# Max-pooling 134 MB through one core: loads first, stores last, issued from GpSimd with the single-packet option

## The chip, the cores and the metric

One core of a Trainium2 chip. The metric is the device time of a run in microseconds (us); the runs of one kernel lie at most 0.26% apart (number 14; 0.18% or less in all others). Besides the run times there is a profile of one run of each kernel; its span is 1.8 to 2.3 us shorter than the time of the run.

## The reference

The input is 32 x 256 x 4096 float32 (134.22 MB). Each row of 4096 is cut into 256 windows of 16 elements, and the largest of each is kept. The output is 32 x 256 x 256 float32 (8.39 MB).

```python
for i in range(output_size):                      # 256
    start = int(i * length / output_size)
    end = int((i + 1) * length / output_size)
    result[:, :, i] = np.max(x[:, :, start:end], axis=-1)
```

That is one pass over memory: 142.6 MB moved, and one VectorE reduction for each of 64 tiles of 128 rows.

## The kernel before

The 8192 rows are 64 tiles of 128 partitions. A ring in SBUF holds nine tiles, and a load brings three, so three loads fit. The output is collected in six buffers of nine tiles each and stored in large pieces. Two stores leave ScalarE's queue amid the loads; five are held back and issued from SyncE after the loads, to give the DMA engines work while VectorE finishes. The last loads get smaller (`LATE`, `PIECES`) so that little is left to reduce after the last byte has come.

```python
RING = 9; G = 9; N_GROUPS = 7; LOAD = 3
LATE = [3, 2, 2, 1, 1]; HELD = 4; PIECES = 4
# ... (views of input and output, buffers)
for g in range(N_GROUPS):
    o = outs[g % len(outs)]
    sizes = LATE if g == N_GROUPS - 1 else [LOAD] * (G // LOAD)
    r = 0
    for n in sizes:
        at = n_read % RING
        nc.sync.dma_start(out=ring[:, at : at + n], in_=xg[g][:, r : r + n])
        for i in range(n):
            nc.vector.reduce_max(out=o[:, (r + i) * O : (r + i + 1) * O],
                                 in_=ring[:, at + i], axis=mybir.AxisListType.X)
        n_read += n
        r += n
    if g < N_GROUPS - 1 - HELD:
        nc.scalar.dma_start(out=og[g], in_=o)
    else:
        held.append((og[g], o))
# ... (the 64th tile in four pieces)
for dst, src in held:
    nc.sync.dma_start(out=dst, in_=src)
nc.scalar.dma_start(out=ol, in_=last_out)
```

## Time and profile before

336.75 us (median of 3 runs, 336.65 to 336.76). What matters of it:

| | before |
|---|---|
| span of the profile | 334.8 us |
| bytes moved | 142.62 MB |
| VectorE busy | 278.8 us |
| three reductions of a load | 13.08 us |
| a load of 6.29 MB at the steady 433 GB/s | 14.5 us |
| first reduction starts | 17.79 us |

The head of the page of the kernel before. A digit is the busy share of one fortieth of the span in tenths; the row GB/s is what DMA moved in it.

```profile
span 334.8 us, 174 instructions
...
DVE  0088989885988959798988989898898988999992
...
DMA  9899999999998999899998999989999999999997
GB/s 370 382 470 446 399 470 393 461 386 439 435 464 382 429 464 464 382 470 423 423 470 376 470 452 393 470 382 464 452 393 470 399 446 431 435 416 411 411 433 315
DMA packets 5041, 142.62 MB, mean 426 GB/s; under 512 B 560, under 2 KB 688, under 8 KB 1200
```

DMA has no empty slice. VectorE (DVE) starts in the third slice and then has a small gap in every load's turn: DMA bounds this kernel, and VectorE needs 10% less time for a load (13.08 us against 14.5).

The chain that ended last of the kernel before, in order of time: start, duration, and what was waited for or run.

```profile
0.66 0.07 issue
0.73 17.04 DMA ring<-in_x_dram
17.77 0.02 issue
17.79 13.08 DVE out L65 x3
30.88 0.02 issue
30.89 30.46 DMA ring<-in_x_dram
```

The first load lands at 17.77 us. Its three reductions end at 30.88, which frees its third of the ring for load 4; that one lands 30.46 us later, because one full load is queued ahead of it. A freed third of the ring thus turns into a request about one load's time before DMA would run out.

Two terms before the next view. A descriptor is one piece of a transfer: the trace shows a load of three tiles as 128 pieces of 48 KB, eight on each of the 16 DMA engines, and calls each of them a packet. A transfer lands when the semaphore that tells of its end has its last update.

The DMA issues of the page before, with the median time from issue to landing in the last column:

```profile
ring<-in_x_dram SPq DMA_DIRECT2D x19, 6144.0 KB, 30.5
...
out_dram<-out ACTq DMA_DIRECT2D x2, 1152.0 KB, 21.5
```

A store of 1152 KB would need 2.7 us alone at 433 GB/s; beside SyncE's loads it needs 21.5 (the median of two), because on each DMA engine its eight descriptors take turns with 48 KB load descriptors, as the packet records show.

### The profile page before, as it was taken

What the parts mean: (1) busy time and instruction counts of PE and PEld (TensorE: products, weight loads), DVE (VectorE), ACT (ScalarE), POOL (GpSimd) and SP (SyncE); (2) the same over time, 40 slices, a digit from 0 to 9 for tenths busy, and PEclk for the clock granted to TensorE, in tenths of its full rate; (3) what the DMA queues carried; (4) which work ended last, traced back from release to release, by engine and by line L of the source; (5) the groups of instructions that cost most, each with busy time, mean ns of one, the idle gap of its engine ahead of it and who ended that gap; (6) DMA issues with size and microseconds to landing.
All of it is one profiled execution on the core that took longest, in us unless ns stands there. A gap on an engine that the chain in (4) does not pass through costs nothing.

```text
span 334.8 us, 174 instructions
## 1 busy us (share of the span) xinstructions
DVE 278.8 (83%) x67; POOL 0.2 (0%) x4
## 2 busy tenths in 40 slices
DVE  0088989885988959798988989898898988999992
POOL 0000000000000000000000000000000000000000
DMA  9899999999998999899998999989999999999997
GB/s 370 382 470 446 399 470 393 461 386 439 435 464 382 429 464 464 382 470 423 423 470 376 470 452 393 470 382 464 452 393 470 399 446 431 435 416 411 411 433 315
DMA packets 5041, 142.62 MB, mean 426 GB/s; under 512 B 560, under 2 KB 688, under 8 KB 1200
## 3 DMA queue, kind: packets, MB, share of 16 engines
q1 hardware_dynamic: 4608, 140.12, 97.4%
q10 hardware_dynamic: 432, 2.49, 1.8%
q14 instruction: 1, 0.01, 0.0%
HBM read 134.22 MB, written 8.39 MB: 426 GB/s over the span
## 4 chain that ended last, share of the span: by engine, by line
DMA 61%; DVE 34%; issue 2%; DVEq 0%
DMA ring<-in_x_dram 61%; DVE out L65 33%; DVE lastout L82 1%; DVEq L119 0%; DVEq L65 0%
## 5 line engine op out<-in xcount | busy, mean ns | idle before, releaser
L65 DVE TENSOR_REDUCE out<-ring 128x256 f32<-128x4096 f32 x63 | 274.3, 4412 | 50.0 <-DMA ring<-in_x_dram 50.0
L82 DVE TENSOR_REDUCE lastout<-ring 128x64 f32<-128x1024 f32 x4 | 4.6, 1208 | 0.0
L105 POOL MEMSET const-bfloat16-1.0<- 128x1 bf16 x1 | 0.1, 102 | 0.0
L105 POOL MEMSET const-uint8-127<- 128x1 uint8 x1 | 0.1, 102 | 0.0
L105 POOL MEMSET const-float32-0.0<- 128x1 f32 x1 | 0.1, 99 | 0.2 <-issue 0.2
L105 POOL MEMSET const-float32-1.0<- 128x1 f32 x1 | 0.1, 99 | 0.0
## 6 DMA issues: line engine op xcount, KB each, us to landing
ring<-in_x_dram SPq DMA_DIRECT2D x19, 6144.0 KB, 30.5
ring<-in_x_dram SPq DMA_DIRECT2D x2, 4096.0 KB, 30.0
out_dram<-out SPq DMA_DIRECT2D x5, 1152.0 KB, 14.8
ring<-in_x_dram SPq DMA_DIRECT2D x2, 2048.0 KB, 30.9
out_dram<-out ACTq DMA_DIRECT2D x2, 1152.0 KB, 21.5
ring<-in_x_dram SPq DMA_DIRECT2D x4, 512.0 KB, 27.8
out_dram<-lastout ACTq DMA_DIRECT2D x1, 128.0 KB, 5.2
```

The lines of the kernel that those rows point to most:

```text
L65: nc.vector.reduce_max(out=o[:, (r + i) * O : (r + i + 1) * O], in_=ring[:, at + i], axis=mybir.AxisListType.X,)
L82: nc.vector.reduce_max(out=last_out[:, cut], in_=ring[:, at, cut], axis=mybir.AxisListType.X)
L105: nc = _bacc.Bacc("TRN2", target_bir_lowering=False, num_devices=1)
```

## The change

Its intent: one queue, so that all loads come before all stores and 19 us of stores (8.39 MB at 433 GB/s) cover the last reductions; large, equal transfers; the option `single_packet=True`; and the first load from SyncE, whose first byte came at 1.74 us. The 64th tile's result goes to a spare part of the ring.

```diff
-    G = 9
-    N_GROUPS = 7
+    G = 21
+    N_GROUPS = 3
     LOAD = 3
-    LATE = [3, 2, 2, 1, 1]
-    HELD = 4
-    PIECES = 4
+    CUT = 15
 ... (buffers; pooled() is the reduce_max of before)
+    def move(dst, src):
+        if n_read == 0:
+            nc.sync.dma_start(out=dst, in_=src)
+        else:
+            nc.gpsimd.dma_start(out=dst, in_=src, single_packet=True)
 ...
     for g in range(N_GROUPS):
 ...
+        for r in range(0, G, LOAD):
             at = n_read % RING
-            nc.sync.dma_start(out=ring[:, at : at + n], in_=xg[g][:, r : r + n])
 ...
+            move(ring[:, at : at + LOAD], xg[g][:, r : r + LOAD])
+            for i in range(LOAD):
+                pooled(outs[g][:, (r + i) * O : (r + i + 1) * O], ring[:, at + i])
+            n_read += LOAD
 ...
+    move(ring[:, at], xl)
+    pooled(spare, ring[:, at])
 ...
-    for dst, src in held:
-        nc.sync.dma_start(out=dst, in_=src)
-    nc.scalar.dma_start(out=ol, in_=last_out)
+    for g in range(N_GROUPS - 1):
+        move(og[g], outs[g])
+    for a, b in ((0, CUT), (CUT, G)):
+        move(og[N_GROUPS - 1][:, a * O : b * O],
+             outs[N_GROUPS - 1][:, a * O : b * O])
+    nc.scalar.dma_start(out=ol, in_=spare)
```

More of the change, by code (lines that the diff above doesn't have):

```diff
@@ L44 @@
         pool.tile([P, G * O], fp32, tag=f"out{i}", name=f"out{i}")
-        for i in range(N_GROUPS - 1)
+        for i in range(N_GROUPS)
     ]
-    last_out = pool.tile([P, O], fp32, tag="lastout", name="lastout")
     main = N_GROUPS * G * P
@@ L53, with pooled @@
     ol = of[main:rows]
+    def pooled(dst, src):
+        nc.vector.reduce_max(out=dst, in_=src, axis=mybir.AxisListType.X)
+    def move(dst, src):
[3 more added lines that the diff above has]
+            nc.gpsimd.dma_start(out=dst, in_=src, single_packet=True)
     n_read = 0
-    held = []
     for g in range(N_GROUPS):
-        o = outs[g % len(outs)]
-        sizes = LATE if g == N_GROUPS - 1 else [LOAD] * (G // LOAD)
-        r = 0
-        for n in sizes:
+        for r in range(0, G, LOAD):
             at = n_read % RING
-            nc.sync.dma_start(out=ring[:, at : at + n], in_=xg[g][:, r : r + n])
-            for i in range(n):
-                nc.vector.reduce_max(
-                    out=o[:, (r + i) * O : (r + i + 1) * O],
-                    in_=ring[:, at + i],
-                    axis=mybir.AxisListType.X,
-                )
-            n_read += n
-            r += n
-        if g < N_GROUPS - 1 - HELD:
-            nc.scalar.dma_start(out=og[g], in_=o)
-        else:
-            held.append((og[g], o))
-    at = n_read % RING
-    oc = O // PIECES
-    for c in range(PIECES):
-        cut = slice(c * oc, (c + 1) * oc)
-        nc.sync.dma_start(out=ring[:, at, cut], in_=xl[:, cut])
-        nc.vector.reduce_max(
-            out=last_out[:, cut], in_=ring[:, at, cut], axis=mybir.AxisListType.X
-        )
-    for dst, src in held:
-        nc.sync.dma_start(out=dst, in_=src)
-    nc.scalar.dma_start(out=ol, in_=last_out)
+            move(ring[:, at : at + LOAD], xg[g][:, r : r + LOAD])
+            for i in range(LOAD):
+                pooled(outs[g][:, (r + i) * O : (r + i + 1) * O], ring[:, at + i])
+            n_read += LOAD
+    at = n_read % RING
+    spare = ring[:, (at + LOAD) % RING].rearrange("p o w -> p (o w)")[:, 0:O]
+    move(ring[:, at], xl)
[3 more added lines that the diff above has]
+    for a, b in ((0, CUT), (CUT, G)):
+        move(
+            og[N_GROUPS - 1][:, a * O : b * O],
+            outs[N_GROUPS - 1][:, a * O : b * O],
+        )
+    nc.scalar.dma_start(out=ol, in_=spare)
 _INS = ['x', 'output_size']
```

## The prediction

> **What bounds it now.** The DMA engines. The page's slices show DMA busy 9 or more tenths nearly everywhere; in the table by stretches 20 to 280 us run at 433 GB/s with a DMA share of 1.00. 142.62 MB at that rate are 329.1 us of a span of 334.8; only 5.7 us are not transfer: the start (the first load, issued at 0.73 us, lands at 17.8; its bytes need 14.5) and a thin end (330 to 335 us: share 0.55). VectorE is second: 64 tiles x 4.41 us = 282 us; the three reductions of a load take 13.1 us, a load 14.5 us.
>
> **What the change can win.** Same bytes, so at most about 5 us. (a) Packets: the trace's packet records show 1815 ns for 49152 B, 347 for 9216 B, 159 for 4096 B. These fit 27.2 GB/s plus about 8 ns a packet; with 288 packets per engine, one packet per transfer might save 2 us (estimate). (b) Tail: the stores (8.39 MB, 19.3 us at 433 GB/s) follow the last load and cover the last reductions (13.2 + 4.4 us), so the end should be dense: 1 to 2 us.
>
> **What it adds.** The first load is on SyncE's queue, eight packets per DMA engine of 1.8 us; loads 2 and 3 come from GpSimd with nothing to wait for[...]. [...] beside ScalarE's first store, 9 KB packets alternate one for one with 48 KB load packets, and a 1.15 MB store needs 21.5 us to land. [...] Load 1, which VectorE wants first, lands last, at about 46.5 us instead of 17.8. The ring holds three loads, so load 4 can't be issued until load 1 is reduced: 46.5 + 13.1 = 59.6, plus 1.5 to start. DMA stands idle about 14.7 us. All of it is on the critical path. Afterwards DMA is continuous: 123.7 MB at 434.5 GB/s = 284.8 us from 61.2, ends at 346.0, plus 0.8 of closing: span 346.8. Measured time is 1.8 above the span: **348.5 us**.
>
> **Other outcome.** [...] there is no hole: about 333 to 335 us. I give this 40%.
>
> Range 332.5 to 351 (it has to cover both). Faster by over 2%: 0.04; within 2%: 0.38; slower: 0.58.
>
> **What would show it.** First reduction's start: about 46 us (right) or 18 us (other outcome), about 31 us if queues alternate by descriptor. A hole of 13 to 15 us in the DMA slices near 46 to 61 us. Steady rate 433 to 435.2 GB/s. Stores alone after the last load, near 420 to 435 GB/s, full to the end.
>
> **What would make it wrong.** A late GpSimd start; arbitration by descriptor; a software queue that is slower than 433 GB/s, or an engine lagging under it, which costs 3.3 us per per cent; stores alone slower than mixed with loads.

The two conditions of the other outcome were other turns or a late GpSimd. The sum: load 1 lands at about 46.5 us, then 13.1 for its reductions and 1.5 to start again give about 61.2; 284.8 for the other bytes gives 346.0, 0.8 of closing 346.8, and 1.8 outside the span 348.5 us. The 46.5 is my estimate, not shown by a trace: three loads of 14.5 us and about 3 us of start (the first load's 17.8 less its 14.5), if load 1 lands last. The 1.5 was an estimate too; number 5 shows 1.53, from the end of load 1's reductions (60.72) to the next packet (62.25).

## The result, and the profile after

337.51 us (median of 6 runs, 337.24 to 337.73) against 336.70 of the kernel before beside it (336.60 to 336.76). The ratio is 1.0023, 95% interval 1.001 to 1.0036: the same within 2%, and slower by a small, certain amount. Ratios here are the mean time of one kernel's runs over that of the other's of the same rounds, so they are not quite the ratio of the medians quoted.

The head of the page after:

```profile
span 335.4 us, 158 instructions
...
DVE  0003999999999999989898898989789898988990
...
DMA  9899899989999999899999999999989999999996
GB/s 369 387 463 457 387 446 399 463 387 463 440 405 469 410 434 463 387 463 434 410 469 393 451 451 393 469 417 428 463 381 469 428 416 463 393 457 399 441 422 271
DMA packets 3889, 142.62 MB, mean 425 GB/s; under 512 B 432, under 2 KB 560, under 8 KB 688
```

There is no hole in the row DMA. VectorE starts a slice later than before and is then full for 13 slices.

The chain after, its first pieces and the load that follows:

```profile
0.74 30.18 DMA ring<-in_x_dram
30.92 0.02 issue
30.94 116.92 DVE out L53 x27
147.86 0.28 issue
148.14 30.04 DMA ring<-in_x_dram
```

The first load, alone on SyncE's queue, lands at 30.92 us. VectorE then runs 27 reductions without a wait. It is late by 13 us and, being about 1.4 us faster per load than DMA, works that off over nine loads. After that the kernel has the old rhythm.

The timeline after, up to 60 us (start, duration, engine, line, instruction; in brackets the idle time before it):

```profile
0.74 0.37 SPq L57 DMA_DIRECT2D ring<-in_x_dram  x1
1.28 1.20 POOL L59 DMA_DIRECT2D ring<-in_x_dram  x2 [0.84 <-PEq L113]
30.94 30.38 DVE L53 TENSOR_REDUCE out<-ring 128x256 f32<-128x4096 f32 x7 [30.94 <-DMA ring<-in_x_dram]
44.31 0.53 POOL L59 DMA_DIRECT2D ring<-in_x_dram  x1 [41.83 <-DVE out L53]
```

GpSimd had issued loads 2 and 3 by 2.5 us, as foreseen. Load 4 went out at 44.31 us; load 3 landed at 47.3. So the next request was there 3 us ahead, and DMA never starved.

The trace's records of single DMA packets show the order on an engine. Strung together by their end and start times (H: a 48 KB descriptor from SyncE's queue, P: one from GpSimd's), the first 24 packets of each of the 16 engines in the kernel after read

```
HHPHPHPHPHPHPHPPPPPPPPPP
```

Each engine took one descriptor from either queue in turn, although P belongs to transfers issued with `single_packet=True`. The first P began at 5.82 us, and the last H ended at 30.55.

Where the rest went shows in four times from those records, placed in the span (us):

| | first byte | last byte | transfer, first to last byte | tail, last byte to end of span |
|---|---|---|---|---|
| before | 1.74 | 333.63 | 331.89 | 1.15 |
| after | 1.74 | 333.20 | 331.46 | 2.15 |

The transfers as a whole became 0.43 us shorter and the tail 1.00 us longer. In the tail after, the trace's instruction records show a drain instruction on GpSimd (one of the program's closing instructions) that ends at 334.63, 1.07 us after the last landing at 333.56; the closing barrier of all engines comes only then. In the kernel before, the barrier follows the last landing directly (334.14 after 333.97). Together the two make the span 0.57 us longer; the measured time differs by 0.81. The profiled runs differ outside the span too: time less span is 1.78 us before and 2.16 after. What that is, the profile does not show. Below it is 2.0 to 2.3 us in the runs that issue most transfers from GpSimd, except in numbers 11 (1.78) and 13 (1.77), which ran on other chips than numbers 1 to 8; so it cannot be read as a price of GpSimd's queue.

The expectations of numbers 3, 4 and 8 count the tail from the last landing instead (0.81 us before, 1.79 after); those from number 9 on count it from the last byte, as the table does.

### The profile page after: what moved, and what is told of

The parts are those of the page before. It is cut to its first block, busy times and chain, and to the rows that moved or that the text cites. A ratio compares the mean times of both kernels' runs of the same rounds, so it can differ in the third digit from the quotient of the medians.

```text
span 335.4 us, 158 instructions
## 1 busy us (share of the span) xinstructions
DVE 278.1 (83%) x64; POOL 13.5 (4%) x29
## 2 busy tenths in 40 slices
DMA packets 3889, 142.62 MB, mean 425 GB/s; under 512 B 432, under 2 KB 560, under 8 KB 688
## 3 DMA queue, kind: packets, MB, share of 16 engines
HBM read 134.22 MB, written 8.39 MB: 425 GB/s over the span
## 4 chain that ended last, share of the span: by engine, by line
DVE 49%; DMA 45%; DVEq 2%; issue 0%
DVE out L53 48%; DMA ring<-in_x_dram 45%; DVEq L113 2%; DVE ring L53 1%
## 5 line engine op out<-in xcount | busy, mean ns | idle before, releaser
L59 POOL DMA_DIRECT2D ring<-in_x_dram x21 | 11.2, 535 | 273.8 <-DVE out L53 273.0
L53 DVE TENSOR_REDUCE ring<-ring 128x256 f32<-128x4096 f32 x1 | 4.4, 4408 | 0.0
L59 POOL DMA_DIRECT2D out_dram<-out x4 | 2.1, 534 | 35.6 <-DVE out L53 35.6
```

What stands on the lines that cost most here:

```text
L53: nc.vector.reduce_max(out=dst, in_=src, axis=mybir.AxisListType.X)
L59: nc.gpsimd.dma_start(out=dst, in_=src, single_packet=True)
```

## The experiments

Theory A, formed on this result: a DMA engine takes turns between two queues one descriptor at a time, and asking for a single packet changes nothing in that. Its rival is the order that I had assumed (load 1 last), or a framing that does something else. Theory C: the lost microsecond is GpSimd's drain. Its rivals are D, a fixed price of using GpSimd's queue at all, and E, a price that grows with the number of its transfers.

### 1. Without the one-packet option

```diff
-            nc.gpsimd.dma_start(out=dst, in_=src, single_packet=True)
+            nc.gpsimd.dma_start(out=dst, in_=src)
```

> The changed kernel without the one-packet option. Theory A (an engine takes turns by descriptor, whatever the framing): nothing moves; first reduction at 31 us, 337.5 us within 0.3, 1815 ns per 48 KB. Rival B (the framing does something, only not what I predicted, for example saves a gap per descriptor): 338 to 340 us, or another order of the first three loads.

Measured: 337.57 us (337.41 to 337.62), first reduction at 30.65 us. Nothing moved beyond 0.3 us. At this size the option is worth nothing, in order or in time.

### 2. First load from GpSimd too

```diff
-        if n_read == 0:
-            nc.sync.dma_start(out=dst, in_=src)
-        else:
-            nc.gpsimd.dma_start(out=dst, in_=src, single_packet=True)
+        nc.gpsimd.dma_start(out=dst, in_=src, single_packet=True)
```

> The changed kernel with the first load from GpSimd too, so one queue for all. Theory A: load 1 is no longer shared with 2 and 3 and lands at 18 to 19 us, VectorE starts 12 us earlier, yet the time hardly moves, because DMA was never idle in the changed kernel: 337.5 to 338.5, the later first byte (about 0.9 us) being all that is lost. Rival (the late first reduction costs time): 2 us or more faster than the changed kernel.

Measured: 338.02 us (337.95 to 338.07). The first byte came at 2.65 us (issue at 1.28) instead of 1.74, and the first reduction began at 19.19 us instead of 30.94. VectorE started 12 us sooner and the kernel ended half a microsecond later: a late start of the engine that has slack cost nothing here. "The first load from SyncE" is worth 0.5 us, less than the 0.92 by which the first byte comes sooner: from first to last byte this run took 331.17 us, 0.29 less than the changed kernel.

### 3. The new order, all from SyncE

```diff
-        if n_read == 0:
-            nc.sync.dma_start(out=dst, in_=src)
-        else:
-            nc.gpsimd.dma_start(out=dst, in_=src, single_packet=True)
+        nc.sync.dma_start(out=dst, in_=src)
```

> The changed order, all from SyncE (last store from ScalarE as in the change). Theory C (the change loses about 1 us at the end because GpSimd's closing drain runs 1.07 us beyond the last landing, and gains 0.4 us of transfer by fewer, larger descriptors): tail after the last byte about 0.8 us, span 334.4, time 336.2 to 336.4, so 0.3 to 0.4 us faster than before. Rival (software issue makes the transfers themselves slower): DMA from first to last byte would shorten below 331.3 us.

Measured: 336.03 us (335.89 to 336.12), ratio to before 0.9979 (0.9967 to 0.9992). First to last byte 331.22 us, tail 1.29 (0.93 from the last landing), span 334.24, time less span 1.79. It beats both kernels, the changed one by 1.5 us. The transfers were 0.24 us shorter than the changed kernel's. By its letter this is the rival's sign (under 331.3), but number 2, where GpSimd issues all loads, has 331.17: software issue does not make the transfers slower. The shorter time goes with one queue at the start: with 48 KB descriptors the runs of this order that begin on one queue have 331.08 to 331.22 (numbers 2, 3, 10), those that begin on two 331.44 to 331.61 (the changed kernel, 1, 4, 11). The tail and the time outside the span make the rest. The page of this kernel:

```profile
DVE  0088989898898989989898898989889898988990
...
DMA  9899898998989989999899998999989999898997
```

VectorE starts in the third slice again. The order is the changed kernel's, only the issuer differs.

### 4. Last piece of the store from SyncE

```diff
-    for a, b in ((0, CUT), (CUT, G)):
-        move(og[N_GROUPS - 1][:, a * O : b * O], ...)
+    move(og2[:, 0 : CUT * O], o2[:, 0 : CUT * O])
+    nc.sync.dma_start(out=og2[:, CUT * O : G * O], in_=o2[:, CUT * O : G * O])
```

> The changed kernel, only the last piece of a store from SyncE, so that GpSimd's last transfer lands about 1.5 us before the end. Theory C: the drain is over before the last landing; tail 0.8 us instead of 1.8, time 336.4 to 336.7. Rival (the second of tail is a fixed price of having used GpSimd's queue at all): 337.4 to 337.6.

Measured: 337.31 us (337.13 to 337.65), tail 1.93. This looks like rival D, but the experiment missed its aim: the piece on SyncE took turns with GpSimd's piece, so GpSimd's last transfer did not land 1.5 us before the end but at 333.56, as late as ever. It decides nothing. Number 11 repairs it.

### 5. SyncE's first load in 8 KB descriptors

```diff
-            nc.sync.dma_start(out=dst, in_=src)
+            nc.sync.dma_start(out=dst, in_=src, max_dma_last_dim=8192)
```

> The changed kernel, only SyncE's first load cut into 8 KB descriptors (48 per engine). Theory A (turn by turn, one descriptor each): load 1 gets 8 KB per turn against 48 KB of loads 2 and 3, so those finish at about 36 us and load 1 last, at about 46 us; load 4 is issued at about 59.5, DMA idles 13 to 15 us, span about 349, time 350 to 352: the hole of my prediction, made by other means. Rival (turns are shared by bytes, or loads 2 and 3 don't matter): load 1 at 31 us or earlier, about 337.5 us.

Measured: 354.49 us (354.19 to 354.56), ratio 1.0527. Load 1 landed at 47.6 us, load 4 was issued at 61.0. In the chain that ended last, load 1 is this piece:

```profile
0.74 46.87 DMA ring<-in_x_dram
```

Stretches of this run (start:end, length, VectorE busy, GpSimd busy, clock, DMA share, GB/s):

```profile
40.00:45.00 5.00, 0.00 (x0) 0.00 (x0) 1.00 1.01 421
45.00:50.00 5.00, 2.36 (x1) 0.00 (x0) 1.00 0.27 110
50.00:55.00 5.00, 5.00 (x2) 0.00 (x0) 1.00 0.00 0
55.00:60.00 5.00, 5.00 (x2) 0.00 (x0) 1.00 0.00 0
60.00:65.00 5.00, 5.00 (x3) 0.53 (x1) 1.00 0.70 246
```

This is the forecast hole: two stretches in which DMA moved nothing while VectorE worked. By the packet records no engine had a packet from 47.19 to 62.25 us, 15.1 us long. Nothing was changed but the size of the first load's descriptors, and with it what this load gets per turn; the packets, strung together as above, again alternate one for one. First to last byte became 348.05 us, 16.6 longer than in the changed kernel. Theory A's times for load 1 and for the issue hold within 1.6 us. Loads 2 and 3 landed at 23.8 and 41.1, not both at about 36: they share a queue and came one after the other, and some ten small descriptors of load 1 went before the first of theirs. The time came out 2.5 us above the range; the hole is at the upper end of what I had put, and where the other 1.5 us of longer transfer come from was not traced.

### 6 and 7. GpSimd's transfers in 8 KB descriptors, with and without the one-packet option

```diff
-            nc.gpsimd.dma_start(out=dst, in_=src, single_packet=True)
+            nc.gpsimd.dma_start(
+                out=dst, in_=src, single_packet=True, max_dma_last_dim=8192   # 7: single_packet=False
+            )
```

> The changed kernel with GpSimd's transfers cut into 8 KB descriptors, 48 per engine[...]. Theory A: load 1 is hardly delayed, 8 x (1.8 + 0.3) + 2 = about 19.5 us. My prediction's mechanism [...] would put it at about 46 us with a hole, over 350 us. Cost of descriptors: if each costs 8 ns whatever the framing, about 40 more per engine and load add 6 to 7 us: 344 us; if the framing saves it, 337.5.

> As the run before, without the one-packet option. Theory A: the same as with it: load 1 at about 19.5 us, about 344 us. If the framing matters for small descriptors, this run and the one before differ, in the landing of load 1 or by several us of time.

Measured: 344.43 us (344.28 to 344.46) with the option, 344.40 (344.20 to 344.51) without. First reduction at 20.26 and 20.54 us. The page of the run with the option:

```profile
DVE  0069989789797978979797897979789797977990
...
DMA  8989999999999999999999999999999999999997
...
DMA packets 17457, 142.62 MB, mean 417 GB/s; under 512 B 432, under 2 KB 560, under 8 KB 1712
```

What VectorE waited for in it: us in total, times, the longest, which is the wait for load 1.

```profile
DVE out L53 <- DMA ring<-in_x_dram: 55.3, 20, 20.3
```

The prediction's order would have put load 1 last, at about 46 us. It landed at 20.2 with the option and at 20.5 without, where theory A's turns of one descriptor each gave about 19.5. The option saves nothing on descriptors either: first to last byte grew by 7.56 us over the changed kernel (339.03 against 331.46). By the packet counts of the two pages an engine had (17457 - 3889) / 16 = 848 descriptors more, so each cost 8.9 ns.

### 8. The kernel before, issued from GpSimd

```diff
-            nc.sync.dma_start(...)      # everywhere
+            nc.gpsimd.dma_start(...)
```

> The kernel before, with everything that SyncE issues moved to GpSimd (the order, pieces and ScalarE stores kept). Theory C: the drain ends the kernel, tail 1.7 to 1.9 us instead of 0.8, and the first byte comes some tenths later: 337.6 to 338.8. Rival (the queue costs nothing, the new order costs): 336.7 within 0.2.

Measured: 339.04 us (339.02 to 339.06), ratio 1.0067. First byte at 2.66, first to last byte 331.85 (before: 331.89), tail 2.24 (1.87 from the last landing, as theory C had), time less span 2.28. The transfers are as fast as from SyncE. The price is 0.92 us at the first byte, 1.09 of tail and 0.50 outside the span; the time came out 0.2 us higher than I had allowed.

### 9. One load in the middle from GpSimd, the rest from SyncE

```diff
-        nc.sync.dma_start(out=dst, in_=src)
+        if n_read == 30:
+            nc.gpsimd.dma_start(out=dst, in_=src)
+        else:
+            nc.sync.dma_start(out=dst, in_=src)
```

> All from SyncE (336.03 us) with one load in the middle moved to GpSimd. Theory C (the second at the end is GpSimd's drain after its own last landing): that landing is 170 us before the end, so the tail stays at 1.2 to 1.3 us and the span at 334.2 to 334.4; time 336.0 to 336.2. Rival D (a fixed price for having used GpSimd's queue at all): tail 2.1 us, time 337 or more.

Measured: 345.90 us (345.71 to 346.34), which neither theory had. The tail is as theory C said, 1.30 us, with the drain over at 166.65, 0.08 us after the one landing. The 10 us have another cause: this run makes the collision in the middle of the kernel, and it changed the order of VectorE's work there.

```profile
150.00:165.00 15.00, 0.00 (x0) 0.00 (x0) 1.00 0.98 423
165.00:175.00 10.00, 8.41 (x2) 0.00 (x0) 1.00 1.06 457
175.00:185.00 10.00, 10.00 (x4) 0.00 (x0) 1.00 0.13 44
```

VectorE's next work in the timeline, with the idle time before it:

```profile
166.59 56.34 DVE L53 TENSOR_REDUCE out<-ring 128x256 f32<-128x4096 f32 x13 [19.03 <-DMA ring<-in_x_dram]
```

SyncE's load issued at 118.5 shared its turns with GpSimd's, issued at 133.3, and landed at 161.7 instead of 149.0 (all from SyncE). In addition the instruction records show that VectorE's program had one reduction of GpSimd's load ahead of those of the load before it, so it waited to 166.59. The third of the ring came free at 184.0. By the packet records the engines had run empty between 176.5 and 177.6, and none had a packet from 177.61 to 184.98.

The collision alone would probably not have made this hole. Had VectorE begun with the load of 161.7, its three reductions (13.08 us) would have freed the third at 174.8, and SyncE's next transfer, 1.0 us from issue to first byte, would have reached the engines at about 175.8, before any ran empty. This is an estimate from the numbers above; no run has the collision without the changed order, and why the built program has that order the record does not show. So two loads that shared the turns made the landing 12.7 us late; that DMA then starved took, by this estimate, the further 9.2 us that VectorE's order cost. At the start of the changed kernel, where VectorE took the loads in order, the request came 3 us before load 3 landed.

### 10. Only the last piece of the store from GpSimd

```diff
     # all from SyncE (number 3), except
+    nc.gpsimd.dma_start(out=og2[:, CUT * O : G * O], in_=o2[:, CUT * O : G * O])
```

> All from SyncE with only the last piece of the stores (0.8 MB) moved to GpSimd, so one transfer, but one of the last to land. Theory C: tail 1.9 to 2.3 us, span 335.0 to 335.4, time 336.9 to 337.4. Rival E (the price grows with the number of GpSimd's transfers, 25 in the changed kernel): 336.1.

Measured: 336.03 us (335.92 to 336.27), tail 1.33. GpSimd's transfer landed at 333.06, among the last, and the drain ended at 333.14. This is rival E's figure. Theory C in its fixed form fell, and so did D.

### 11. Both last pieces from SyncE

```diff
-    for a, b in ((0, CUT), (CUT, G)):
-        move(og[N_GROUPS - 1][:, a * O : b * O], ...)
+    for a, b in ((CUT, G), (0, CUT)):
+        nc.sync.dma_start(out=og2[:, a * O : b * O], in_=o2[:, a * O : b * O])
```

> The changed kernel, with both pieces of the last group's store from SyncE, the piece that is ready last first, so that GpSimd's last transfer lands some 4 us before the end. Theory C: GpSimd's drain is over before SyncE's last landing, tail 1.2 to 1.3 us, time 336.4 to 336.8. Rival D: tail 2.1, time 337.5.

Measured: 336.17 us (335.99 to 336.20), ratio 0.9983, tail 1.24. GpSimd issued 23 transfers, the last landed at 331.87, and its drain ran 0.99 us more, to 332.86. SyncE's and ScalarE's last landings are at 333.24 and 333.56, so the drain hid behind them. This is the changed kernel with two transfers moved, and 1.3 us faster, from different rounds and 0.2 us better than I had put. In the profiled runs 0.91 of it is tail; 0.38 lies outside the span, and as this run was on another chip than number 1, the changed kernel but for the option, that part need not come from the edit. The lag is there, but here it cost only as far as it outlasted the last landing of all the queues (in number 4 it did, though GpSimd's was not the last).

### 12. The first store amid the loads

```diff
     # all from SyncE, except, after the last tile of group 0:
+        if g == 0:
+            nc.scalar.dma_start(out=og[0], in_=outs[0])
     # ... (its store after the loads is left out)
```

> All from SyncE, but the first 2.75 MB store leaves from ScalarE as soon as it is reduced, amid the loads. If the loads-first order is worth something by itself: loads end 6.3 us later, the last reductions at about 333 us and the last small store lands after them with little left to cover it: 337.5 to 339. Rival (order is worth nothing here, DMA is busy either way): 336.0 within 0.2.

Measured: 337.75 us (337.60 to 337.79). The last reduction ended at 333.2, the small last store was issued at 333.26 and landed at 334.97, when everything else had landed by 333.44. The packet records have no gap amid the loads, and one at the end, from 333.03 to 334.11. So loads first is worth 1.7 us in this version (336.03 of number 3, from other rounds). The kernel before got the same cover in another way, with five held stores and ever smaller last loads; that is probably why the change gains almost nothing by it.

### 13. One row per transfer

```diff
-    LOAD = 3
+    LOAD = 1
```

> The changed kernel with one row (16 KB descriptors) per transfer, so 67 transfers from GpSimd instead of 25. Rival E (about 43 ns of drain per GpSimd transfer): the drain ends 2.8 to 3.0 us after GpSimd's last landing, tail about 4 us. Theory C (fixed): 1.0 to 1.1 us after, tail 2.2. Either way the smaller descriptors add 16 per engine and three rows, 21 times, at 8 ns: about 2.7 us of transfer. Time with E about 342, with C about 340.

Measured: 341.97 us (341.81 to 342.10). GpSimd issued 67 transfers, and the drain ended 2.78 us after the last landing. First to last byte is 334.52, which is 3.06 longer than the changed kernel's. Rival E's figure again. Over the runs, the lag of the drain against GpSimd's number of transfers:

| run | transfers from GpSimd | drain's end after their last landing, us |
|---|---|---|
| 9, 10 | 1 | 0.08 |
| 11 | 23 | 0.99 |
| 4 | 24 | 1.03 |
| changed kernel, 1, 5 | 25 | 1.07 |
| 2 | 26 | 1.11 |
| 8 | 32 | 1.35 |
| 13 | 67 | 2.78 |
| 6, 7 (8 KB descriptors) | 25 | 0.46 |

The first seven rows lie on 0.04 us plus 0.041 per transfer. The last row does not. Its loads have six times the descriptors, and why its lag is smaller was not tested.

### 14. The middle load from ScalarE

```diff
         if n_read == 30:
-            nc.gpsimd.dma_start(out=dst, in_=src)
+            nc.scalar.dma_start(out=dst, in_=src)
```

> All from SyncE with one load in the middle from ScalarE. If two hardware queues take turns by descriptor just as SyncE's and GpSimd's did: the load before it, issued at 118.5, lands at about 162 instead of 149 us, VectorE waits for both, and the time is 345 to 347 as with GpSimd. Rival (only the software queue pushes in): 336.0 to 336.3.

Measured: 345.66 us (345.39 to 346.28). The load before it landed at 161.8, not at 149.0 as in number 3, and VectorE waited 18.8 us, again for the later of the two loads first, as in number 9. Taking turns does not belong to the software queue; ScalarE's queue does it too.

## Why the prediction was wrong

The measured 337.5 us lies inside the wide range, but the forecast was 348.5 and "slower", and that was wrong. That it lies inside is no merit: the range had to cover two outcomes, and the measured time is neither of them.

**The step that failed** reads: "Load 1, which VectorE wants first, lands last, at about 46.5 us instead of 17.8." It rested on an assumption of mine about the order of turns, which no trace showed, and on my reading of the diff that a transfer goes as a single packet. The runs showed one descriptor of each in turn. Load 1 needs eight turns, load 2 too, so they landed at 30.9 and 32.7 us and load 3 at 47.3. Load 1 was indeed late, by 13 us, but not by 29. Numbers 1, 6 and 7 show no trace of such a packet: with the option and without it the first reduction began at 30.94 and 30.65 us (48 KB descriptors), and at 20.26 and 20.54 (8 KB). Whether the framing is not made, or made and not honoured in the order of turns, these runs cannot tell.

**What followed from it was right.** Number 5 gave load 1 the late landing by other means: 47.6 us (foreseen 46.5), load 4 at 61.0, an empty DMA, and a time 17 us longer. The chain "load 1 late, ring full, DMA idle" held there. Its input was false. In total the prediction's own steps would have fallen 6 us short of number 5 (348.5 against 354.5): its transfers began again 1.1 us later than foreseen, took 287.6 us from there and not 284.8, and the tail and the time outside the span were 1.7 us longer.

**The other outcome was mis-sized as well.** I gave it 333 to 335 us. Three terms were off:

- (a) "one packet per transfer might save 2 us (estimate)": 0 us (numbers 1, and 6 against 7). The 8 ns of the fit, 8.9 in number 6, are paid for each descriptor.
- (b) "Tail: ... 1 to 2 us": the last byte came 0.43 us sooner. I read the low share of the last 5 us as an idle end, but the packet records show transfers up to 333.63 of 334.78, and the held stores already did the covering (number 12 shows what the cover is worth).
- The missing term: GpSimd's drain, 1.07 us after its last landing. I did not look for it, since no GpSimd transfer stood in the profile of before.

**Right:** DMA bounds the kernel; the steady rate stays at 433 GB/s with software issue; and the start of VectorE was the right thing to look at, with "about 31 us if queues alternate by descriptor" as the sign of what happened.

**Where the gain of the change went.** Its order and larger descriptors are worth 0.7 us (336.03 from SyncE against 336.72 of before in the same rounds). Issuing the first load from SyncE and the rest from GpSimd costs 1.5 us (337.51 against 336.03, from different rounds; 337.57 in number 1, in the same rounds): in the profiled runs 0.86 of tail, 0.24 of transfer, which goes with the two queues at the start, and 0.37 outside the span, the last unexplained.

## What to carry to other kernels

Where two queues had large transfers in flight at once, a load landed late by what it gave the other: at 30.9 us in the changed kernel, where the one queue of number 3 had the first reduction start at 18.3, and at 161.7 instead of 149.0 in number 9. Keep transfers that are needed in order on one queue (in number 3 the first three loads' reductions began at 18.3, 32.8 and 47.3 us, in order), or work out from the descriptor sizes who lands when and whether the next request is still issued in time. Look also at the order in which the built program uses the loads: in numbers 9 and 14, by estimate, it made the late landing dear. A late start of the engine with slack cost nothing where DMA never ran out of requests (in number 2 VectorE started 12 us sooner, and the time was 0.5 us longer); in number 5, where DMA stood empty for 15.1 us, the time was 17 us longer. Let a queue with little to do after its last landing end the kernel: GpSimd's drain ran 1.07 us past it in the changed kernel, and here two stores moved from GpSimd to SyncE were worth 0.9 us of tail.
